# Adding four partial sums of a value row by loads that accumulate, in place of two products with a matrix of ones

## The chip, the cores and the metric

The kernel runs on one core of a Trainium2 chip. The metric is the device time of one launch in microseconds (us), lower is better. Before the change three runs took 2063.79, 2063.28 and 2062.68 us, a median of 2063.28.

## The reference, cut to what matters

One inference step of a two-layer decoder: layer A mixes tokens with a gated MLP, layer B with attention; each also has two half-weight SwiGLU blocks (the FFNs) and a gated input embedding. Everything is float32. Between the layers one shared K and V is made from the residual stream, for 512 prompt rows and for 32 "sample" rows (8 sequences of 4 new tokens). The change concerns only the sample rows of V:

```python
def shared_kv(h, kv_norm, w_kvf, b_f, k_norm):
    xs = rmsnorm(h, kv_norm)
    kvf = xs @ w_kvf
    ...
    v = kvf[..., D_ATT:2 * D_ATT].reshape(bsz, L, N_HEADS, HEAD_DIM)
    ...
k_sample, v_sample, logf_sample   # outputs; v_sample is 32 x 1024
```

`v_sample` is an output, and the attention of layer B reads it again.

## The kernel before, in words

The residual stream lies in SBUF as 8 chunks of 128 features by 544 tokens (512 prompt and 32 sample tokens side by side). A float32 product is made of three products in float32r: ScalarE (ACT) rounds an operand to its high part (line 198 for weights, 285 for activations, 297 with a gain), VectorE (DVE) subtracts to get the low part (199, 286, 298), and TensorE (PE) adds high x high (241), high x low (245) and low x high (247). Weights arrive in 512 KB blocks. All loads and stores sit in one queue in program order, SyncE's (SP), and a transfer that has to wait there keeps everything behind it waiting. A block of weights is split into its two parts two blocks ahead of its use.

The method `kv` makes K, V and the forget values. For V it goes through four groups `g` of 256 columns. In each group the prompt rows are made with the three products (829 to 831). The 32 sample rows are made in plain float32 beside them (840): for each of the 8 chunks a product with 32 rows of output, and chunk `k` writes the rows from `32 * (k % 4)` of one PSUM tile, so that four chunks fill 128 rows and the next four add to them. What stands there is four partial sums of 32 rows each; ACT copies it, times the norm, into `box["sv"]` (844). After the last group the four partial sums have to be added.

Before the change that is a product with a matrix in the constants, `C_SUM`, which has a one where the row number modulo 32 equals the column: two products of 512 columns each into PSUM tiles `t` (881), each copied by ACT into the tile `vs` (882). Two stores follow: to the output `vs` (883) and to a scratch `vsd` in device memory (884), which attention loads half a millisecond later (1260).

Behind `kv` comes the first FFN of layer B. It starts with four "plain" tiles of PE (lines 241 to 247, each copied out by 426), while ACT and DVE still make the forms of the activations (307, 311, 313, 314, 285, 286). Then it goes over to a scheme of seven products for eight (491, 24 matmuls each, order 1, 5, 6, 2, 7, 3, 4) in an order written out by hand; its evictions are lines 499 to 513, and the gate is 451 to 457. The weights of a pair of column blocks are four quarters, loaded in the order of line 165 as first to fourth; the fourth is used alone in product 2, and in the sums (line 184) for the products 3. Around the change the order within each engine comes from a scheduler that simulates the kernel.

Of the kernel before, what the change touches and what calls it, by code (L numbers as in the profile page):

```python
# [22 lines left out]
F32 = mybir.dt.float32  # L23
# [3 lines left out]
ALU = mybir.AluOpType  # L27
AX = mybir.AxisListType

P = 128  # L30
D = 1024
# [4 lines left out]
NS = NB * NQ  # L36
# [41 lines left out]
C_ID, C_ROLE, C_B4, C_H, C_SEL, C_NEGQ, C_TRI4, C_SUM = 0, 128, 140, 144, 152, 156, 160, 192  # L78
# [16 lines left out]
class Builder:  # L95
# [672 lines left out]
    def kv(self, h, box, ffn_gain):  # L768

        nc, o = self.nc, self.o  # L770
# [11 lines left out]
        box = {}  # L782
# [15 lines left out]
        def columns():  # L798

            t = self.pb()  # L800
            for j in range(4):
                nc.tensor.matmul(t[:, j:j + 1], rstd[:, j * P:(j + 1) * P], self.ident[:, 0:1], start=True, stop=True)
            for j in range(4):
                nc.tensor.matmul(t[32 * j:32 * j + 32, 4:5], rstd[:, SEQ:], self.ident[:, 0:1], start=True, stop=True,
                                 skip_group_check=True)
            box["rc"] = self.sm(5)
            nc.scalar.copy(box["rc"], t[:, 0:5])
# [61 lines left out]
        for step in KV_ORDER:  # L869
            head, _, rest = step.partition(":")  # L870
            if head == "c":
                columns()
            elif head:
                v_group(int(head[1]), parse(rest))
            else:
                for run in parse(rest)[0]:
                    run()
        vs = self.big()[:NS, :, :512]
        for a in range(2):
            t = self.pb()  # L880
            nc.tensor.matmul(t[:NS, :], self.c[:, C_SUM:C_SUM + NS], box["sv"][:, 512 * a:512 * a + 512], start=True, stop=True)
            nc.scalar.copy(vs[:, a, :], t[:NS, :])
        nc.sync.dma_start(out=o["vs"].rearrange("t (a n) -> t a n", a=2), in_=vs)
        nc.sync.dma_start(out=self.vsd[:].rearrange("t (a n) -> t a n", a=2), in_=vs)
        return nxt, rstd
# [632 lines left out]
```

## Time and profile before

| | |
|---|---|
| median of the three runs | 2063.28 us |
| the profiled execution, its own time | 2064.12 us |
| its span | 2062.4 us |
| DVE busy | 1507.2 us (73%) |
| ACT busy | 950.4 us (46%) |
| POOL (GpSimd) busy | 184.2 us (9%) |
| moved by DMA | 237.95 MB, mean 115 GB/s |

The page cuts the span into 40 slices of 51.6 us; the digits are tenths. The place of the change, around 1080 us, is at the end of slice 21, where DMA has one of its peaks: this is where V and K are stored and the next FFN's weights are fetched.

```profile
PE   8999999999999999999999999999999999999999
ACT  7534344423554344454456343534365754344451
POOL 0000000410100000043060000001141200000020
PEclk9999999999999999999999999999999999999999
DMA  5233234212223222432374323314669222222431
```

The granted clock of TensorE is full in every slice.

### The profile page before, as it was taken

What the parts mean: (1) busy time and instruction counts of PE and PEld (TensorE: products, weight loads), DVE (VectorE), ACT (ScalarE), POOL (GpSimd) and SP (SyncE); (2) the same over time, 40 slices, a digit from 0 to 9 for tenths busy, and PEclk for the clock granted to TensorE, in tenths of its full rate; (3) what the DMA queues carried; (4) which work ended last, traced back from release to release, by engine and by line L of the source; (5) the groups of instructions that cost most, each with busy time, mean ns of one, the idle gap of its engine ahead of it and who ended that gap; (6) DMA issues with size and microseconds to landing.
All of it is one profiled execution on the core that took longest, in us unless ns stands there. A gap on an engine that the chain in (4) does not pass through costs nothing.

```text
span 2062.4 us, 38838 instructions
## 1 busy us (share of the span) xinstructions
PE 2042.4 (99%) x16432; PEld 2012.4 (98%) x16432; DVE 1507.2 (73%) x1861; ACT 950.4 (46%) x1421; POOL 184.2 (9%) x222
## 2 busy tenths in 40 slices
PE   8999999999999999999999999999999999999999
PEld 8999999999999999999999999999987999999999
DVE  7877777556687778776688777786476888777773
ACT  7534344423554344454456343534365754344451
POOL 0000000410100000043060000001141200000020
PEclk9999999999999999999999999999999999999999
DMA  5233234212223222432374323314669222222431
GB/s 185 84 110 107 74 109 141 97 44 83 83 92 113 73 105 80 154 99 82 107 255 162 113 85 110 105 69 136 193 204 323 99 99 85 100 103 82 130 97 44
DMA packets 93823, 237.95 MB, mean 115 GB/s; under 512 B 9538, under 2 KB 27490, under 8 KB 93650
## 3 DMA queue, kind: packets, MB, share of 16 engines
q1 hardware_dynamic: 93506, 235.44, 34.1%
q8 instruction: 129, 2.11, 0.4%
q14 instruction: 44, 0.36, 0.1%
q10 hardware_dynamic: 144, 0.04, 0.0%
HBM read 218.95 MB, written 16.49 MB: 114 GB/s over the span
## 4 chain that ended last, share of the span: by engine, by line
PE 92%; DVE 3%; ACT 2%; issue 1%; DMA 1%; POOL 0%; SPq 0%; DVEq 0%; ACTq 0%; POOLq 0%
PE ps L491 33%; PE ps L241 16%; PE ps L247 16%; PE ps L245 16%; PE pb L491 5%; DVE big L199 1%; ACT big L198 1%; PE ps L1272 1%; PE ps L1268 1%; PE ps L1271 1%; ACT big L285 0%; DVE big L184 0%; DVE big L286 0%; PE ps L1223 0%; PE ps L829 0%
## 5 line engine op out<-in xcount | busy, mean ns | idle before, releaser
L491 PE MATMUL ps<-big,big 128*128 128x272 f32 x5616 | 727.7, 288 | 1.8 <-DVE big L508 1.3
L491 PEld LDWEIGHTS ps<-big,big 128*128 128x128 f32 x5616 | 714.2, 188 | 2.4 <-issue 1.6
L199 DVE TENSOR_TENSOR big<-big,big 128x1024 fp32r<-128x1024 f32 (+2 forms) x538 | 591.9, 1103 | 105.5 <-ACT big L198 105.0
L198 ACT CAST big<-big 128x1024 fp32r<-128x1024 f32 (+2 forms) x538 | 488.0, 932 | 267.6 <-DVE big L184 262.8
L241 PE MATMUL ps<-big,big 128*128 128x256 f32 (+1 forms) x2684 | 558.8, 289 | 7.6 <-ACT big L198 7.6
L247 PE MATMUL ps<-big,big 128*128 128x256 f32 x2684 | 554.9, 289 | 1.5 <-DVE big L199 1.5
L245 PE MATMUL ps<-big,big 128*128 128x256 f32 x2684 | 554.0, 287 | 0.0
L241 PEld LDWEIGHTS ps<-big,big 128*128 128x128 f32 x2684 | 430.9, 189 | 11.3 <-ACT big L198 8.5
L247 PEld LDWEIGHTS ps<-big,big 128*128 128x128 f32 x2684 | 429.8, 188 | 3.1 <-DVE big L199 2.7
L245 PEld LDWEIGHTS ps<-big,big 128*128 128x128 f32 x2684 | 432.5, 189 | 0.0
L326 POOL TENSOR_TENSOR st<-st,tmp 128x544 f32<-128x544 f32 (+1 forms) x63 | 87.5, 1388 | 1587.7 <-ACT tmp L324 1587.5
L530 DVE SCALAR_TENSOR_TENSOR big<-ps,big 128x544 f32<-128x544 f32 x160 | 115.6, 723 | 106.5 <-PE ps L247 106.4
L184 DVE TENSOR_TENSOR big<-big,big 128x1024 f32<-128x1024 f32 x156 | 190.2, 1219 | 0.0
L499 ACT COPY tmp<-ps 128x544 f32<-128x544 f32 x117 | 71.7, 613 | 141.2 <-PE ps L491 141.2
L454 ACT ACTIVATE big<-big 128x544 f32<-128x544 f32 x88 | 58.0, 660 | 163.2 <-DVE big L451 162.0
L491 PE MATMUL pb<-big,big 128*128 128x272 f32 x936 | 124.0, 288 | 0.0
L451 DVE TENSOR_TENSOR big<-big,st 128x1088 f32<-128x1088 f32 x88 | 113.4, 1290 | 10.6 <-ACT big L513 8.8
L491 PEld LDWEIGHTS pb<-big,big 128*128 128x128 f32 x936 | 120.2, 188 | 0.0
L286 DVE TENSOR_TENSOR big<-big,big 128x544 fp32r<-128x544 f32 (+1 forms) x112 | 82.1, 739 | 36.4 <-ACT big L285 36.3
L297 ACT ACTIVATE big<-big,gains 128x544 fp32r<-128x544 f32 (+1 forms) x80 | 55.8, 704 | 104.6 <-DVE big L530 64.9
L298 DVE SCALAR_TENSOR_TENSOR big<-big,gains,big 128x544 fp32r<-128x544 f32 (+1 forms) x80 | 65.8, 830 | 25.8 <-ACT big L297 25.8
L285 ACT CAST big<-big 128x544 fp32r<-128x544 f32 (+1 forms) x112 | 71.3, 644 | 17.8 <-DVE big L457 9.0
(208 smaller groups left out, 1430.8 us busy)
## 6 DMA issues: line engine op xcount, KB each, us to landing
big<-in_w SPq DMA_DIRECT2D x156, 512.0 KB
big<-in_w2a SPq DMA_DIRECT2D x64, 512.0 KB
big<-in_w2b SPq DMA_DIRECT2D x32, 384.0 KB
big<-in_w13p SPq DMA_DIRECT2D x16, 512.0 KB
big<-in_win SPq DMA_DIRECT2D x16, 512.0 KB
big<-in_wg SPq DMA_DIRECT2D x16, 512.0 KB
big<-in_ck SPq DMA_DIRECT2D x16, 512.0 KB
big<-in_cv SPq DMA_DIRECT2D x16, 512.0 KB
```

The lines of the kernel that those rows point to most:

```text
L184: self.nc.vector.tensor_tensor(t, a, b, ALU.add if op == "+" else ALU.subtract)
L198: self.nc.scalar.copy(hi, src)
L199: self.nc.vector.tensor_tensor(lo, src, hi.bitcast(F32), ALU.subtract)
L241: i = nc.tensor.matmul(out[:, a:b], wh, xh[:, a:b], start=s, stop=False)
L245: nc.tensor.matmul(out[:, a:b], wh, xl[:, a:b], start=False, stop=False)
L247: nc.tensor.matmul(out[:, a:b], wl, xh[:, a:b], start=False, stop=e)
L286: self.nc.vector.tensor_tensor(pair[:, 1, cols], src, pair[:, 0, cols].bitcast(F32), ALU.subtract)
L326: nc.gpsimd.tensor_tensor(acc[:, cols], acc[:, cols], sq, ALU.add)
L451: tt(g, g, rstd.unsqueeze(1).broadcast_to([P, 2, T]), ALU.mult)
L491: nc.tensor.matmul(dst[w], a[:, c], b, start=k in "152" and kp == 0 and n == 0, stop=kp == NKP - 1 and n == 2, skip_group_check=True)
L499: nc.scalar.copy(t["r" + k], t["C" if k == "5" else "A"])
L530: nc.vector.scalar_tensor_tensor(h[c], whole(out), 0.5, h[c], ALU.mult, ALU.add)
```

## The change

The two products and the two copies go. The 128 rows of `box["sv"]` are stored to a new scratch `vparts` in device memory (512 KB, SP's queue). GpSimd (POOL) then loads its four pieces of 32 rows into `vs`, one on the other: the first load overwrites, the three behind it add what they read to what is there. The stores of `vs` stay as they were.

```diff
         vs = self.big()[:NS, :, :512]
-        for a in range(2):
-            t = self.pb()
-            nc.tensor.matmul(t[:NS, :], self.c[:, C_SUM:C_SUM + NS], box["sv"][:, 512 * a:512 * a + 512], start=True, stop=True)
-            nc.scalar.copy(vs[:, a, :], t[:NS, :])
+        part = self.dram.tile([P, D], F32, name="vparts")
+        nc.sync.dma_start(out=part[:], in_=box["sv"])
+        for k in range(4):
+            src = part[NS * k:NS * k + NS, :].rearrange("t (a n) -> t a n", a=2)
+            nc.gpsimd.dma_start(out=vs, in_=src, **({"accum_op": ALU.add} if k else {}))
         nc.sync.dma_start(out=o["vs"].rearrange("t (a n) -> t a n", a=2), in_=vs)
         nc.sync.dma_start(out=self.vsd[:].rearrange("t (a n) -> t a n", a=2), in_=vs)
```

On ACT, at the end of `kv`, the program has these rows; minus marks what only the kernel before has (`big_12213` and `big_12218` are parts of V, `big_12223` is `vs`, `big_12233` the first form of the FFN's activations).

```order
 L285 CAST big_12213<-big_12038 128x512
 L285 CAST big_12218<-big_12038 128x512
-L882 COPY big_12223<-pb_12224 32x512
-L882 COPY big_12223<-pb_12227 32x512
 L307 ACTIVATE big_12233<-big_88,gains 128x544 x2
 L285 CAST big_12238<-tmp_12236 128x544
```

The two copies are gone and everything behind them moves up; no other row of ACT moves. DVE's rows are the same in both kernels. On PE the two products are gone, and the first two plain tiles are woven into each other a little differently.

On SP, at the same place, the kernel before has these rows (`big_12251`, `12321`, `12323` and `12325` are the first to fourth quarter of the first weights for the seven products; `12530` and `12568` belong to the next).

```order
L896 DMA kd<-big_12072 256x1x512
L896 DMA kd<-big_12120 256x1x512
L847 DMA out_v<-big_12038 128x512 x2
L849 DMA vd<-big_12213 256x1x512
L849 DMA vd<-big_12218 256x1x512
L883 DMA out_vs<-big_12223 64x1x512
L884 DMA vsd<-big_12223 64x1x512
L165 DMA big_12251<-in_w 128x1024
L165 DMA big_12321<-in_w 128x1024
L165 DMA big_12323<-in_w 128x1024
L165 DMA big_12325<-in_w 128x1024
L165 DMA big_12530<-in_w 128x1024
```

The changed kernel has these in their place (its line numbers are two higher behind the change).

```order
L898 DMA kd<-big_12072 256x1x512
L881 DMA vparts<-big_11362 128x1024
L898 DMA kd<-big_12120 256x1x512
L847 DMA out_v<-big_12038 128x512 x2
L849 DMA vd<-big_12213 256x1x512
L849 DMA vd<-big_12218 256x1x512
L165 DMA big_12251<-in_w 128x1024
L165 DMA big_12321<-in_w 128x1024
L165 DMA big_12323<-in_w 128x1024
L885 DMA out_vs<-big_12223 64x1x512
L886 DMA vsd<-big_12223 64x1x512
L165 DMA big_12325<-in_w 128x1024
```

The store of the partial sums stands between the two stores of K, and the two stores of `vs` have moved behind the first three quarters, ahead of the fourth. POOL has the four loads between its last copy of K's sample columns (line 893 before) and its next work, the sums of squares of line 326 at the end of the FFN.

## The prediction

> **What bounds the kernel now.** I read the page first, for the engine that sets the time.
>
> ```profile
> span 2062.4 us, 38838 instructions
> PE 2042.4 (99%) x16432; PEld 2012.4 (98%) x16432; DVE 1507.2 (73%) x1861; ACT 950.4 (46%) x1421; POOL 184.2 (9%) x222
> PE 92%; DVE 3%; ACT 2%; issue 1%; DMA 1%; POOL 0%; SPq 0%; DVEq 0%; ACTq 0%; POOLq 0%
> ```
>
> PE is busy all the time and holds 92% of the chain that ended last. So time saved on PE is worth its full size where PE is not about to wait, and nothing where it waits for another engine next. Which of the two holds at 1080 us is read from the timeline of PE, here around the two removed products (line 881) and at its next waits.
>
> ```profile
> 1063.87 1.07 PE L840 MATMUL pb<-big,xraw 128*32 128x256 f32 x16
> 1064.87 0.39 PE L829 MATMUL ps<-big,big 128*128 128x256 f32 x1
> ...
> 1076.51 1.07 PE L840 MATMUL pb<-big,xraw 128*32 128x256 f32 x16
> 1077.39 1.02 PE L881 MATMUL pb<-big,consts 128*32 128x512 f32 x2
> 1078.35 0.52 PE L241 MATMUL ps<-big,big 128*128 128x256 f32 x2
> ...
> 1080.46 0.41 PE L247 MATMUL ps<-big,big 128*128 128x256 f32 x2
> 1080.80 1.04 PE L881 MATMUL pb<-big,consts 128*32 128x512 f32 x2
> 1081.78 0.52 PE L241 MATMUL ps<-big,big 128*128 128x256 f32 x2
> 1082.13 0.42 PE L245 MATMUL ps<-big,big 128*128 128x256 f32 x2
> 1082.39 0.42 PE L247 MATMUL ps<-big,big 128*128 128x256 f32 x2
> ...
> 1092.04 0.52 PE L241 MATMUL ps<-big,big 128*128 128x256 f32 x2 [0.24 <-ACT big L198]
> ...
> 1100.03 0.52 PE L247 MATMUL ps<-big,big 128*128 128x256 f32 x2 [0.49 <-DVE big L199]
> ...
> 1105.61 9.23 PE L491 MATMUL ps<-big,big 128*128 128x272 f32 x72
> 1114.67 3.19 PE L491 MATMUL pb<-big,big 128*128 128x272 f32 x24
> ```
>
> PE runs through until 1092.04, where the third plain tile waits 0.24 us for the high part of its weights from ACT. The reader is to see that PE has almost no slack there: whatever makes PE faster before 1092 turns into a longer wait for ACT. From 1105.61 on PE runs without a wait through the first seven products. So the worth of the change is set by when ACT is done, and the timelines of ACT and of DVE show what that hangs on.
>
> ```profile
> 1085.25 1.14 ACT L285 CAST big<-big 128x512 fp32r<-128x512 f32 x2
> 1086.30 1.04 ACT L882 COPY big<-pb 32x512 f32<-32x512 f32 x2
> 1087.25 1.39 ACT L307 ACTIVATE big<-big,gains 128x544 f32<-128x544 f32 x2
> 1088.67 0.73 DVE L311 TENSOR_TENSOR tmp<-big 128x544 f32<-128x544 f32 x1 [1.47 <-ACT big L307]
> 1089.43 0.65 ACT L285 CAST big<-tmp 128x544 fp32r<-128x544 f32 x1 [0.79 <-DVE tmp L311]
> 1090.93 1.05 ACT L198 CAST big<-big 128x1024 fp32r<-128x1024 f32 x1
> 1092.02 1.23 DVE L199 TENSOR_TENSOR big<-big,big 128x1024 fp32r<-128x1024 f32 x1 [0.23 <-ACT big L198]
> ```
>
> That is a closed chain: the copies of line 882, the forms of line 307, DVE's 311 that waited 1.47 us for them, ACT's 285 that waited for it, the cast 198, and PE. The removed copies are links of it.
>
> **The change part by part.** *The two products.* A group of line 840 normally takes 1064.87 - 1063.87 = 1.00 us to the next product; with the first removed product in between it takes 1078.35 - 1076.51 = 1.84, so 0.84 goes. A step from one pair to the next is 1082.39 - 1082.13 = 0.26; with the second in between it is 1081.78 - 1080.46 = 1.32, and the pair behind it starts 0.35 later instead of 0.26, so 1.06 + 0.09 = 1.15 goes. PE gains 1.99 us. On its own that is worth nothing, since PE would stand at 1092 that much longer.
>
> *The two copies.* ACT's next instruction starts 1087.25 - 1086.30 = 0.95 us earlier. It needs nothing that moves with PE: 285 before it runs back to back with its predecessors, and the plain tiles that ACT copies out later are done 1.99 us earlier. So the chain above arrives 0.95 us earlier, PE takes up 0.95 of its 1.99 us, and waits 0.24 + 1.04 us instead of 0.24. The later wait, 1100.03, hangs on the same two engines and moves along. **The term is -0.95 us.** The different weaving of the first two tiles on PE issues the same products.
>
> *The store of the partial sums.* SP issues it behind the store of K at 1079.03, and its last piece is there when ACT has written it:
>
> ```profile
> 1078.86 0.46 ACT L844 ACTIVATE big<-pb,sm 128x256 f32<-128x256 f32 x1
> ...
> 1079.03 4.84 SPq L896 DMA_DIRECT2D kd<-big  x2
> 1087.90 0.82 SPq L883 DMA_DIRECT2D out_vs<-big  x1
> 1088.77 1.24 SPq L884 DMA_DIRECT2D vsd<-big  x1
> 1090.06 2.55 SPq L165 DMA_DIRECT2D big<-in_w  x5
> ...
> 1100.00 0.33 SPq L165 DMA_DIRECT2D big<-in_w  x1
> ```
>
> So it starts at about 1079.6. How long until it has landed, no row shows; the rows below bound it. They are windows of the DMA engines (their share is the last but one column, GB/s the last) and two transfers from the chain of waits.
>
> ```profile
> 1080.00:1085.00 5.00, 5.00 (x34) 4.01 (x34) 4.57 (x8) 4.33 (x9) 0.00 (x0) 1.00 0.99 361
> 1095.00:1100.00 5.00, 4.54 (x37) 4.32 (x35) 4.69 (x8) 4.97 (x7) 0.00 (x0) 1.00 0.75 300
> 1102.00:1103.00 1.00, 1.00 (x11) 1.00 (x10) 0.24 (x1) 0.73 (x1) 0.00 (x0) 1.00 0.77 307
> 1103.00:1104.00 1.00, 1.00 (x11) 1.00 (x10) 0.65 (x1) 0.32 (x1) 0.00 (x0) 1.00 0.04 16
> ...
> 1058.66 7.83 DMA tmp<-rows
> ...
> 1091.70 5.98 DMA big<-in_w
> ```
>
> A load of the same 512 KB that is alone, issued at 1100.00, is through by 1103.1 (the window behind it moves nearly nothing): 3.1 us. In the full stretch one took 5.98, and 272 KB behind a full queue 7.83. DMA is full at 1080 (0.99), so I take the upper end, 7.4, and the store has landed at 1087.0; the bounds are 1082.7 and 1087.4. Its 0.52 MB delay the loads behind it by at most 0.52 MB / 361 GB/s = 1.5 us, but the two stores of `vs`, 0.26 MB, no longer stand ahead of the first three quarters, and DVE did not wait for these three when it summed two of them at 1101:
>
> ```profile
> 1099.89 1.22 DVE L199 TENSOR_TENSOR big<-big,big 128x1024 fp32r<-128x1024 f32 x1
> 1101.02 1.22 DVE L184 TENSOR_TENSOR big<-big,big 128x1024 f32<-128x1024 f32 x1
> ```
>
> The load with 5.98 us, the fourth of the group, had landed by 1097.7, so there are over 3 us of cover; this costs nothing.
>
> *The four accumulating loads* are a chain: each waits for the one before it, since it adds to what that one wrote. POOL itself has nothing else queued until the end of this FFN, so nothing waits behind them there. Their duration `d` is the unknown; no load on POOL's queue is in the trace. From below, 128 KB alone takes a quarter of 3.1, 0.8 us; from above, 7.83. Nearest are 3.1 (alone) and 5.98 (in the full stretch) for four times the bytes. Three of them fall into the stretch that is full until about 1099, where 5.98 less three quarters of the bytes' own time (0.39 MB / 323 GB/s at 5.98 us, an estimate of 1.2) is 4.8; the last falls behind it, 3.1 - 1.2 = 1.9. I take d = (3 x 4.8 + 1.9) / 4 = 4.1 and the chain ends at 1087.0 + 16.4 = **1103.4**.
>
> *The wait that is added.* SP waits for that end at the first store of `vs`, and behind it in the queue stand the second store, the fourth quarter of the weights, and all that follow. In the kernel before, the fourth quarter was issued with the group of five at 1090.06; now it leaves about 1 us after the chain's end (two stores to issue, 0.82 and 1.24 us in a full queue, less in an empty one), moves behind 0.26 MB of stores (0.9 us at 307 GB/s) and takes 3.1 itself: it has landed 5.0 us after the chain's end, at 1108.4. Who waits for it is in these rows of ACT:
>
> ```profile
> 1106.32 2.00 ACT L198 CAST big<-big 128x1024 fp32r<-128x1024 f32 x2
> 1108.82 0.61 ACT L499 COPY tmp<-ps 128x544 f32<-128x544 f32 x1 [0.51 <-PE ps L491]
> ```
>
> The second cast of the pair, at 1107.27, reads the fourth quarter; moved up by 0.95 it wants it at 1106.3. So ACT and DVE stand for about 2.1 us. PE does not use that quarter before product 2, at 1114.67 - 0.95 = 1113.7, and the first thing that it misses is another: the copy of line 499 behind the cast. It saves product 1 before product 6 adds to the same PSUM tile. A product takes (1114.67 - 1105.61) / 3 = 3.02 us, so product 6 starts at 1105.61 + 6.04 - 0.95 = 1110.7; the cast and the copy take 0.95 + 0.61, so PE loses nothing as long as the quarter has landed by 1109.1, the chain has ended by **1104.1**, and d is at most 4.3. My 4.1 leaves 0.2 us per load: the cover is thin. The loads behind the fourth quarter are used later than it, and catch up.
>
> [...]
>
> **The sum** is -0.95 us against the profiled execution's own 2064.12 us. That lies 0.84 above the median of the runs shown, 2063.28, so in the runs it is 2063.28 - 0.95 = **2062.3**.
>
> **Rivals.** *The late quarter (slower).* If d is over 4.3 us, PE waits before product 6, and each 0.1 us of d costs 0.4: at d = 5.98 the stall is 4 x (5.98 - 4.3) = 6.7, net +5.8, 2069.1; at 7.83 it is 14.1, net +13.2, 2076.5. For it: DMA is full until 1099, and POOL has to prepare each load. Against it: POOL's queue does not stand behind SP's, and a load is a quarter of the size.
>
> *DVE holds POOL up.* The change is the first to let POOL make up transfers, and if POOL could not while a DVE operation of the kind at 1092.02 runs, each load would wait for the rest of one, at most 1.23 us: d = 4.1 + 1.2 = 5.3, a stall of 4.0, net +3.1, 2066.4. Against it: all DVE operations in this stretch are of two tensor inputs, and no row shows POOL held by them. [...]
>
> *PE's whole gain.* If ACT could be early by itself, PE's 1.99 us would count: 2061.3. The wait of 1.47 us for ACT's 307 speaks against it.
>
> *Nothing.* ACT and DVE stand for some microseconds and a later product takes the 0.95 us back: 2063.3.
>
> **How the numbers follow.** Chances: forecast 0.53, late quarter 0.27, DVE holds POOL 0.06, PE's whole gain 0.05, nothing 0.09. The smallest difference that a measurement of this kernel tells from no change is about 0.2%, 4.1 us. Faster by that no case gives; I leave 0.03 for what I have not seen. Slower by that needs a net of +4.1, a stall of 5.1 and d over 5.6: about half of the late quarter, 0.13. The rest, 0.84, is within. The range goes from PE's whole gain less the runs' half spread (2061.3 - 0.6 = 2060.7) to the late quarter at d = 5.98, 2069.1; it leaves out the rest of that rival and the 0.03. The likeliest case's own range is 2061.3 to 2063.3.
>
> **What would show each step.** PE's 1092.04 at about 1091.1 with a wait of 1.3 us for ACT's 198 shows the first term; POOL's four loads and the end of the last one show d; the issue of SP's first store of `vs` shows the chain's end; ACT's second cast of the pair waiting for a DMA shows the late quarter, and a wait of PE's 491 for ACT's 499 or of line 198 shows the loss. I am wrong if ACT's forms do not start earlier, or if the four loads take more than 17 us together.

## The result, and the profile after

| | before | after |
|---|---|---|
| median | 2063.38 us (19 runs) | 2066.52 us (19 runs, 2065.39 to 2068.38) |
| ratio after to before | | 1.0015, interval 1.0008 to 1.0021 |
| the profiled execution, its own time | 2064.12 us | 2065.79 us |
| its span | 2062.4 us | 2064.0 us |

The change makes the kernel slower by 3.1 us (1.7 to 4.3 by the interval). From the page of the changed kernel, its span and the engines:

```profile
span 2064.0 us, 38840 instructions
PE 2040.6 (99%) x16428; PEld 2011.7 (97%) x16428; DVE 1507.0 (73%) x1861; ACT 949.5 (46%) x1419; POOL 187.8 (9%) x226
```

PE has 1.8 us less work and the span is 1.6 us longer: PE lost more by waiting than it gained. What it waits for stands in the list of PE's waits (us in total, how often, the longest), here two rows of it, of the kernel before and then of the changed one:

```profile
PE ps L241 <- ACT big L198: 7.6, 3, 7.1
...
PE ps L491 <- ACT tmp L499: 0.5, 1, 0.5
```

```profile
PE ps L241 <- ACT big L198: 8.5, 3, 7.2
PE ps L491 <- ACT tmp L499: 2.6, 3, 1.5
```

The first row grew by 0.9. In front of the third plain tile the wait went from 0.24 to 1.01 us, so 0.77 of it is there, PE's own gain waited away; the rest lies in the first wait of the launch (its longest, 7.1 and 7.2). The wait of line 491 for line 499 grew by 2.1: new waits among the products of seven. The timeline of PE after the change shows where they are:

```profile
1090.43 0.52 PE L241 MATMUL ps<-big,big 128*128 128x256 f32 x2 [1.01 <-ACT big L198]
...
1104.00 6.20 PE L491 MATMUL ps<-big,big 128*128 128x272 f32 x48
1111.69 3.30 PE L491 MATMUL ps<-big,big 128*128 128x272 f32 x24 [1.49 <-ACT tmp L499]
...
1118.65 6.29 PE L491 MATMUL ps<-big,big 128*128 128x272 f32 x48 [0.64 <-ACT tmp L499]
1125.43 12.26 PE L491 MATMUL ps<-big,big 128*128 128x272 f32 x96 [0.48 <-DVE big L508]
1137.53 3.16 PE L491 MATMUL pb<-big,big 128*128 128x272 f32 x24
```

In the kernel before, all these products ran without a wait. These rows follow those that the prediction shows:

```profile
1117.70 18.20 PE L491 MATMUL ps<-big,big 128*128 128x272 f32 x144
1135.74 3.16 PE L491 MATMUL pb<-big,big 128*128 128x272 f32 x24
```

Two executions do not start this stage at the same moment, so a fixed point ahead of the change is needed. DVE's first operation of line 311 in this stage is one: it precedes all that the copies touch. Here it is in the kernel before, and then after the change, there with the rows in which ACT and DVE miss the fourth quarter:

```profile
1079.62 0.71 DVE L311 TENSOR_TENSOR tmp<-big 128x544 f32<-128x544 f32 x1
```

```profile
1078.97 0.71 DVE L311 TENSOR_TENSOR tmp<-big 128x544 f32<-128x544 f32 x1
...
1110.08 1.05 ACT L198 CAST big<-big 128x1024 fp32r<-128x1024 f32 x1 [4.32 <-DMA big<-in_w]
1111.03 0.61 ACT L499 COPY tmp<-ps 128x544 f32<-128x544 f32 x1
...
1111.16 1.23 DVE L199 TENSOR_TENSOR big<-big,big 128x1024 fp32r<-128x1024 f32 x1 [4.14 <-DMA big<-in_w]
```

The whole stage stands 0.65 us earlier in this execution (1079.62 - 1078.97), and the first product of seven 1.61 (1105.61 - 1104.00), so 0.96 is gained up to there. The last product shown is 1.79 later instead (1137.53 - 1135.74): 3.40 us were lost on the way, and 2.44 net. (The three waits of PE shown above add up to 2.61 only, because a wait counts from the modelled end of the row before it; the starts of the rows hold the whole loss.) ACT and DVE stand for over 4 us before a transfer, and PE waits for the copy 499 behind it. Why the quarter is late is to be read on POOL's and SP's timelines:

```profile
1087.65 0.78 POOL L884 DMA_DIRECT2D big<-vparts  x1 [10.98 <-DMA vparts<-big]
1094.38 0.86 POOL L884 DMA_DIRECT2D big<-vparts  x1 [5.95 <-DMA big<-vparts]
1097.91 0.81 POOL L884 DMA_DIRECT2D big<-vparts  x1 [2.68 <-DMA big<-vparts]
1101.82 0.81 POOL L884 DMA_DIRECT2D big<-vparts  x1 [3.10 <-DMA big<-vparts]
...
1079.89 0.93 SPq L881 DMA_DIRECT2D vparts<-big  x1
...
1087.23 2.66 SPq L165 DMA_DIRECT2D big<-in_w  x3
1104.96 0.66 SPq L885 DMA_DIRECT2D out_vs<-big  x1
...
1106.31 4.00 SPq L165 DMA_DIRECT2D big<-in_w  x5
```

SP issues three quarters at 1087.23, then stands until the fourth load has landed, 1104.96, and only then issues the two stores and the fourth quarter. The store of the partial sums took 1087.65 - 1079.89 = 7.8 us; the loads, from one issue to the next, 6.73, 3.53, 3.91 and, to SP's store, 3.14, together 17.3.

### The profile page after: what moved, and what is told of

Read it like the earlier page. It is cut to its first block, busy times and chain, and to the rows that moved or that the text cites. A ratio compares the mean times of both kernels' runs of the same rounds, so it can differ in the third digit from the quotient of the medians.

```text
span 2064.0 us, 38840 instructions
## 1 busy us (share of the span) xinstructions
PE 2040.6 (99%) x16428; PEld 2011.7 (97%) x16428; DVE 1507.0 (73%) x1861; ACT 949.5 (46%) x1419; POOL 187.8 (9%) x226
## 4 chain that ended last, share of the span: by engine, by line
PE 92%; DVE 3%; ACT 2%; DMA 1%; issue 1%; POOL 0%; SPq 0%; ACTq 0%; DVEq 0%; POOLq 0%
PE ps L491 32%; PE ps L241 16%; PE ps L247 16%; PE ps L245 16%; PE pb L491 5%; DVE big L199 1%; ACT big L198 1%; PE ps L1274 1%; PE ps L1270 1%; PE ps L1273 1%; DVE big L184 1%; PE ps L1225 0%; PE ps L829 0%; PE ps L830 0%; ACT big L285 0%
```

## The experiments

**Theory.** The loss is the late quarter: its place in SP's queue behind a wait for the loads. **Rivals:** the added traffic, or DVE held up by POOL's making up the transfers (POOL's four rows of them last 0.78 to 0.86 us each); and, for the size of the gain, that PE's own 1.99 us count.

All runs were timed against the kernel before on the same chip. The table has, from the timelines, the start of DVE's first 311 of the stage, of the first product of seven (491) and of the last 491 block shown above, and the distance from the 311 to the two.

| kernel | median us | ratio to before, interval | 311 | first 491 | last block | 311 to first 491 | 311 to last block |
|---|---|---|---|---|---|---|---|
| before | 2063.4 to 2063.5 | | 1079.62 | 1105.61 | 1135.74 | 25.99 | 56.12 |
| the change | 2066.52 | 1.0015 (1.0008 to 1.0021) | 1078.97 | 1104.00 | 1137.53 | 25.03 | 58.56 |
| e1, stores by POOL | 2062.34 | 0.9996 (0.9987 to 1.0005) | 1079.60 | 1104.64 | 1134.77 | 25.04 | 55.17 |
| e9, the same again | 2062.64 | 0.9998 (0.9989 to 1.0007) | 1078.34 | 1103.38 | 1133.51 | 25.04 | 55.17 |
| e2, traffic only | 2063.59 | 0.9999 (0.9990 to 1.0008) | 1079.17 | 1105.16 | 1135.30 | 25.99 | 56.13 |
| e7, two loads | 2065.83 | 1.0013 (1.0004 to 1.0023) | 1078.66 | 1103.71 | 1136.28 | 25.05 | 57.62 |
| e3, no sum | 2063.46 | 1.0000 (0.9991 to 1.0009) | 1077.91 | 1102.96 | 1133.09 | 25.05 | 55.18 |
| e5, products only | 2063.55 | 0.9999 (0.9990 to 1.0008) | 1078.68 | 1103.72 | 1133.85 | 25.04 | 55.17 |
| e6, copies only | 2064.10 | 1.0004 (0.9995 to 1.0013) | 1079.32 | 1107.00 | 1137.13 | 27.68 | 57.81 |
| e8, POOL copies | 2065.14 | 1.0008 (0.9999 to 1.0017) | 1079.96 | 1105.84 | 1135.97 | 25.88 | 56.01 |

**e1 and e9: the stores of `vs` on another queue.** POOL issues them behind its loads; SP does not wait for these, and its next eight loads of weights stand in one row, from 1087.86 on.

```diff
-        nc.sync.dma_start(out=o["vs"].rearrange("t (a n) -> t a n", a=2), in_=vs)
-        nc.sync.dma_start(out=self.vsd[:].rearrange("t (a n) -> t a n", a=2), in_=vs)
+        nc.gpsimd.dma_start(out=o["vs"].rearrange("t (a n) -> t a n", a=2), in_=vs)
+        nc.gpsimd.dma_start(out=self.vsd[:].rearrange("t (a n) -> t a n", a=2), in_=vs)
```

> The changed kernel, but the two stores of the summed rows are issued by POOL behind the four loads, so SP's queue does not wait for them; on SP the fourth quarter of the weights stands right behind the third again. Theory 'late quarter' (the loss comes only from SP waiting for the chain of loads ahead of the fourth quarter): ACT's second cast does not wait for a DMA, no stall of PE behind 1104, and the 0.95 us of the removed copies are left: 2063.4 - 0.95 = 2062.4. Rival 'traffic' (the loss comes from 1 MB more of transfers in a stretch where DMA is full): the same bytes move, so the time stays at about 2066.5. Rival 'POOL' (making up the transfers holds DVE up): also about 2066.5.

> The changed kernel with the two stores of vs issued by POOL, a second time, to settle the size of its gain: 2062.3 if the first term is real and the late quarter the only loss (first run 2062.34), 2063.4 if the first run was noise.

The loads and their traffic are as in the change, and the loss is gone: 2062.34 and 2062.64, as the late quarter has it. POOL's, ACT's and PE's timelines of e1:

```profile
1106.56 0.55 POOL L885 DMA_DIRECT2D out_vs<-big  x1 [2.45 <-DMA big<-vparts]
...
1105.35 2.00 ACT L198 CAST big<-big 128x1024 fp32r<-128x1024 f32 x2
...
1104.64 9.23 PE L491 MATMUL ps<-big,big 128*128 128x272 f32 x72
...
1116.73 18.20 PE L491 MATMUL ps<-big,big 128*128 128x272 f32 x144
```

The loads end even later here, at 1106.56 (the 311 stands 0.63 later than in the change), but ACT's pair of casts runs through without a wait, and none of PE's products of seven waits. This version is some 4 us faster than the change. Against the kernel before it shows 1.1 and 0.9 us less; both intervals take in no change, so it is not shown to beat that kernel, though the stage itself is 0.95 shorter in both profiles.

**e2: the traffic alone.** The kernel before, with the store and the four loads added into a buffer that nobody reads.

```diff
+        vx = self.big()[:NS, :, :512]
+        part = self.dram.tile([P, D], F32, name="vparts")
+        nc.sync.dma_start(out=part[:], in_=box["sv"])
+        for k in range(4):
+            src = part[NS * k:NS * k + NS, :].rearrange("t (a n) -> t a n", a=2)
+            nc.gpsimd.dma_start(out=vx, in_=src, **({"accum_op": ALU.add} if k else {}))
```

> The kernel before, with its products, copies and stores, and beside them the store of the partial sums and the four accumulating loads into a tile that nobody reads. Theory 'late quarter': nobody waits for these transfers, so the time is that of before, 2063.4 within 0.5. Rivals 'traffic' and 'POOL': 3.1 us from the changed kernel plus the 0.95 that the copies cost here, 2067.5.

2063.59, and the stage has the length of before to 0.01 us. Neither the bytes nor POOL's work beside DVE cost anything here. Both rivals of the loss would have made it 2067.5, which lies above the interval (up to 2065.0), and they fall. Whether the loads themselves take longer because of DVE this run cannot tell, since nobody waits for them.

**e7: a shorter chain in a worse place.** Two loads instead of four, so two of the four partial sums are left out.

```diff
-        for k in range(4):
+        for k in range(2):
```

> The changed kernel with two of the four loads, so two of the four partial sums are left out. The chain is then 7 us shorter, but the scheduler puts the two stores of the sum behind the first quarter of the weights on SP, so the second and third quarter wait for it. By the trace of the changed kernel the chain ends at 1097.9, the third quarter lands at about 1104.3, and DVE, which wants to sum it at 1099.4, waits 4.9 us. Theory 'late quarter' (what counts is where the wait stands in SP's queue and who needs what is behind it): PE loses 2 to 3.5 us again, 2064.5 to 2066. Rivals 'traffic' and 'POOL' (what counts is the number of loads): about half of the changed kernel's loss of 4.1, 2064.5 at most, and no wait of DVE for a DMA.

SP's, DVE's and PE's timelines:

```profile
1086.91 0.82 SPq L165 DMA_DIRECT2D big<-in_w  x1
1096.36 0.66 SPq L885 DMA_DIRECT2D out_vs<-big  x1
...
1102.97 1.23 DVE L184 TENSOR_TENSOR big<-big,big 128x1024 f32<-128x1024 f32 x1 [3.77 <-DMA big<-in_w]
...
1110.27 3.30 PE L491 MATMUL ps<-big,big 128*128 128x272 f32 x24 [0.36 <-ACT tmp L499]
...
1117.41 6.29 PE L491 MATMUL ps<-big,big 128*128 128x272 f32 x48 [0.81 <-ACT tmp L499]
```

The chain ends 8.3 us sooner than in the change (1104.96 - 1096.36, less the 0.31 by which this execution stands earlier at the 311), but the scheduler, which knows that it is shorter, has put the stores behind the first quarter, so that three quarters wait instead of one. The loss stays: 2065.83. The time alone would not rule out the rivals' 2064.5, which the interval just takes in, but DVE's wait of 3.77 us for a quarter does; the late quarter had put it at 4.9. What counts is what stands behind the wait, not how much is loaded.

**e3: no sum at all.** Products and copies go, and nothing comes in their place.

```diff
-        vs = self.big()[:NS, :, :512]
-        for a in range(2):
...
+        vs = box["sv"][:NS, :].rearrange("t (a n) -> t a n", a=2)
```

> The kernel before without the two products and the two copies, and without anything in their place: the stores take the first 32 rows of the partial sums, so the addition of the four sums is left out. This is the whole gain there is. By the first term of the prediction (ACT's two copies lie in the chain, PE's own time does not count): -0.95, 2062.4. If PE's own 1.99 us count: 2061.4. If later waits take it back: 2063.4.

A miss: 2063.46, no gain in the median, although the stage is 0.95 shorter from the 311 on. The interval, 1.9 us to each side, takes in a gain of 0.95 as well as none, so the runs alone cannot tell. The next two were made to find out more.

**e5: the products alone,** without the copies.

```diff
-        vs = self.big()[:NS, :, :512]
+        vs = box["sv"][:NS, :].rearrange("t (a n) -> t a n", a=2)
         for a in range(2):
...
-            nc.scalar.copy(vs[:, a, :], t[:NS, :])
```

> The kernel before without the two copies on ACT; the two products with the matrix of ones stay on PE and nobody reads them, and the stores of vs take the first of the four partial sums straight from box["sv"] (the addition is left out). My theory, that the copies are worth 0.95 us through ACT and PE's products nothing: the first seven-product matmul 0.9 to 1.0 us earlier against line 840's last, and 2062.4 us. Rival (PE's own work counts): no gain, 2063.4. If the place gains 0.95 and the time does not, as in the run without products and copies, the gain is lost again later.

The stage is 0.95 shorter with the products still on PE: the copies are the gain, PE's 1.99 us are not. But again the median shows none, 2063.55. Half a millisecond later the scheduler has exchanged two rows on DVE, in e3, e5 and e8 alike and in no other kernel of the table: in attention a reciprocal stands ahead of the next reduction. DVE and then PE, first of the kernel before, then of e5:

```profile
1506.04 0.87 DVE L1123 TENSOR_REDUCE sm<-ps 128x1 f32<-128x256 f32 x2
...
1509.26 0.44 PE L1105 MATMUL ps<-big,big 128*128 128x384 f32 x1 [0.49 <-ACT tmp L1124]
```

```profile
1504.15 0.41 DVE L1122 TENSOR_REDUCE sm<-ps 128x1 f32<-128x256 f32 x1
1505.18 0.16 DVE L1124 RECIPROCAL sm<-sm 128x1 f32<-128x1 f32 x1 [0.63 <-ACT tmp L1123]
1505.26 0.54 DVE L1122 TENSOR_REDUCE sm<-ps 128x1 f32<-128x384 f32 x1
...
1508.16 0.46 PE L1104 MATMUL ps<-big,big 128*128 128x384 f32 x1 [1.27 <-ACT tmp L1123]
```

The reciprocal waits for ACT, the reduction that could run stands behind it, and PE waits 1.27 us instead of 0.49. Counted from the 311, which stands 0.94 earlier in e5, the first row of DVE is 0.95 earlier than before, and PE's row only 0.16. That gives 0.8 of the 0.95 back. In e1, whose rows are not exchanged, the same product of PE stands at 1508.29 with a wait of 0.48, still 0.95 earlier. It is read from the profiles; none of the three kernels was run with the two rows put back.

**e6: the copies alone,** from SBUF instead of PSUM, without the products.

```diff
-            t = self.pb()
-            nc.tensor.matmul(t[:NS, :], self.c[:, C_SUM:C_SUM + NS], box["sv"][:, 512 * a:512 * a + 512], start=True, stop=True)
-            nc.scalar.copy(vs[:, a, :], t[:NS, :])
+            nc.scalar.copy(vs[:, a, :], box["sv"][:NS, 512 * a:512 * a + 512])
```

> The kernel before without the two products on PE; the two copies on ACT stay, but copy the first of the four partial sums from SBUF (the addition is left out). My theory: PE's 1.99 us turn into a longer wait for ACT at the third plain tile (0.24 + 1.99 = about 2.2 us, less what the copies themselves move), the first seven-product matmul where it was, 2063.4 us. Rival (PE's whole gain): 2061.4.

Not only is PE's whole gain absent (2064.10; 2061.4 lies below the interval): the stage, expected as long as before, is 1.69 us longer. PE's timeline, then the windows (the last but two column is the granted clock, then DMA's share and GB/s):

```profile
1091.83 0.82 PE L241 MATMUL ps<-big,big 128*128 128x256 f32 x2 [2.39 <-ACT big L198]
...
1097.79 0.66 PE L241 MATMUL ps<-big,big 128*128 128x256 f32 x2
1098.24 0.46 PE L245 MATMUL ps<-big,big 128*128 128x256 f32 x2
...
1092.00:1095.00 3.00, 3.00 (x12) 2.69 (x13) 2.43 (x3) 2.71 (x5) 0.00 (x0) 0.50 0.98 384
...
1098.50:1101.00 2.50, 2.50 (x22) 2.50 (x21) 2.46 (x3) 0.96 (x2) 0.00 (x0) 1.00 0.13 23
```

PE waits 2.39 us, about the 2.2 that were expected, and then runs at half its clock until about 1098.3, a pair in 0.45 us instead of 0.25. In this execution PE's saved work is worth less than nothing, because it turns into a wait behind which PE runs at a granted clock of 0.50. The runs alone, with an interval that takes in no change, do not show the loss.

**e8: the buffer kept.** POOL copies the first partial sum into `vs`, so that buffers rotate as before.

```diff
+        nc.gpsimd.tensor_copy(vs, box["sv"][:NS, :].rearrange("t (a n) -> t a n", a=2))
```

> No products and no copies on ACT; POOL copies the first of the four partial sums into vs, so that the buffers rotate as in the kernel before and only PE's and ACT's rows differ (the addition is left out). If the 0.95 us are real and the run without a vs buffer lost them through other buffers or by noise: 2062.4. If the gain is always lost again after the FFN: 2063.4.

Both expectations missed: 2065.14. The experiment brought a cost of its own, seen on POOL's and DVE's timelines:

```profile
1079.73 1.20 POOL L879 COPY big<-big 32x1024 f32<-32x1024 f32 x1 [2.07 <-ACT big L844]
...
1079.96 1.55 DVE L311 TENSOR_TENSOR tmp<-big 128x544 f32<-128x544 f32 x1
```

The 311 takes 1.55 us instead of 0.71 while POOL copies. Of the 25.88 in the table 0.84 is that; without it 25.04 is left, as in e1, e3, e5 and e9. And it has the exchanged rows in attention. The shorter stage (0.11) and the exchange (0.8) together make 0.7 of the 1.6 us by which its median lies above the kernel before; the rest has no cause shown, and its interval takes in no change. So it does not decide whether a changed rotation of buffers costs anything; that stays open.

## Why the prediction was wrong, step by step

The forecast was 0.95 us less than before, 2062.3; the runs show 3.1 more, 2066.5. That this lies inside the range is no merit of the likeliest case: the range went up to 2069.1 for the late quarter's sake. Two steps failed. The chain of loads was to end at 1103.4, with 0.7 us of cover, and it ended 2.2 later: this turned a gain into a loss. And one stall was to be the whole loss, with everything catching up behind it: this made the loss 3.4 us instead of 1.5. The runs also told the two kernels apart at 0.15%, where the prediction took 0.2% for the smallest difference that they could.

**The first term was right in place and size.** From the 311 to the first product of seven 0.95 was forecast; 0.96 was measured, and in six of the seven kernels without the copies the distance lies between 25.03 and 25.05 against 25.99 (the seventh, e8, has a cost of its own). PE's row at 1092.04 came as foretold, at 1090.43 (0.65 of the difference is the offset), with a wait of 1.01 for line 198 instead of 1.28. That the products themselves are worth nothing is shown by e5, which keeps them and gains the same.

**The end of the chain was the step that failed.** On the clock of the kernel before (0.65 added) it was put at 1103.4 and came at 1105.61. Of the 2.2 us, 1.3 lie in the store of the partial sums, which landed at 1088.3 instead of 1087.0: it was issued 0.9 later than assumed and took 7.8 instead of 7.4. The other 0.9 lie in the loads, 17.3 us instead of 16.4. That their mean, d = 4.33, is so near the 4.1 is luck in part: the four errors, +1.9, -1.3, -0.9 and +1.2, cancel for the most part. The first load, issued 0.4 us behind the three quarters (1087.23), took 6.73 instead of 4.8. The next two took less than 4.8, and the stretch that I took for full was not: the change itself held the fourth quarter and what follows back, as a window of the DMA engines shows (share 0.41, 64 GB/s). The last took 3.14 instead of 1.9.

```profile
1095.00:1100.00 5.00, 4.51 (x36) 4.30 (x35) 4.69 (x7) 3.56 (x5) 1.04 (x2) 1.00 0.41 64
```

**The bound was right.** PE was to lose nothing if the chain ended by 1104.1, that is if the loads took no more than 17 us. The chain ended 1.5 later, and PE's first new wait is 1.49. Quarter and chain were 5.0 apart in the forecast and are 5.1 in the trace (1110.08 - 1104.96).

**The size of the loss was not.** After the stall at product 6 the prediction had everything catch up, since the loads behind are used later. The loads did: up to the last product shown, ACT and DVE have no second wait for a DMA. DVE did not. Of the kernel before, these windows lie behind the stall (behind the length come the busy times of PE, of its weight loads and of DVE, each with its count):

```profile
1117.00:1123.00 6.00, 6.00 (x50) 6.00 (x50) 6.00 (x8) 2.43 (x3) 0.00 (x0) 1.00 0.08 32
...
1129.00:1135.00 6.00, 6.00 (x51) 6.00 (x50) 5.87 (x8) 4.07 (x7) 0.00 (x0) 1.00 0.00 0
```

DVE is busy for 6.00 and 5.87 of 6 us there, and for 5.96 in the window between them. What it stood for before the quarter it cannot make up there. Its operation 508, for which PE waits at 1125.43, shows it, before and then after the change:

```profile
1121.99 0.72 DVE L508 TENSOR_TENSOR big<-ps,tmp 128x544 f32<-128x544 f32 x1
```

```profile
1124.56 0.72 DVE L508 TENSOR_TENSOR big<-ps,tmp 128x544 f32<-128x544 f32 x1
```

With the 0.65 that is 3.2 us later, long behind the stall, and PE ran into it again, at 1118.65 (there through ACT's 499) and at 1125.43. The loss became 3.4 us instead of 1.5, and -0.95 + 3.4 = +2.4 in the profiles beside +3.1 in the runs, whose interval takes in 2.4. By the prediction's own sum the measured end of the chain would have given only -0.95 + 1.5 = +0.55.

**The rivals.** That the traffic, or POOL's work beside DVE, costs time by itself is excluded by e1 and e2. "DVE holds POOL up" is another thing, longer loads, and no run tests it alone. Its price for a load, 5.3, is not what the last three took, 3.53, 3.91 and 3.14, although DVE was busy for 4.69 of 5.00 us in the window above; for the first, with 6.73, it stays open beside the traffic of the three quarters. That its time, 2066.4, is so near the measured one is chance. No run shows that the two tensor inputs of DVE's operations speak against it, as the prediction had it: such an operation did run 0.84 us longer beside a copy of POOL (e8). "PE's whole gain" is excluded by e5 and e6. "Nothing" had the right picture of an engine that stands and hands its lateness on, but took it for smaller than the gain. The late quarter was the right one, and e1 shows it by its removal; its chance of 0.27 was too low for a bound with 0.7 us of cover on a sum of two unseen durations.

## What to carry to other kernels

When a transfer's data come from a slow chain, look at what stands behind it in the same in-order queue, and give such a store a queue on which nobody waits: here that alone was worth 4 us. A cover that is thinner than the spread of the durations it rests on is no cover: here 0.7 us, with loads between 3.14 and 6.73. A stall of an engine that has no idle time behind it was handed on at later places as well, here 3.4 us instead of 1.5 with DVE busy for 5.87 to 6.00 of 6 us in the kernel before, so look at that engine's share in the windows after the stall. When a small edit is timed under a scheduler, compare the order of rows in the whole program, since it can exchange two rows half a millisecond away and give most of the gain back there, 0.8 of 0.95 us in e5.

## What the runs showed that was not expected

Behind a wait of PE of 2.39 us (e6) the granted clock was 0.50 for some 6 to 7 us: it is 1.00 in the window from 1089 to 1091.5, 0.50 in those from 1092 to 1095 and from 1095 to 1098, and 1.00 again in that from 1098.5 to 1101. After 1.49 in the changed kernel (1.00 from 1111.7 to 1118) and after 1.65 in e8 (1.00 from 1092.3 to 1098), whose row stands here, no such stretch followed:

```profile
1092.26 0.52 PE L241 MATMUL ps<-big,big 128*128 128x256 f32 x2 [1.65 <-ACT big L198]
```

It is one wait in one execution, and the runs do not show from what length of a wait on this happens, or whether the length decides it.

While POOL copied for 1.20 us in e8, DVE's 311 took 1.55 us instead of 0.71, so 0.84 longer; it began 0.97 us before the copy's end. Through it the copy held up the chain that PE waits for: 25.88 us from the 311 to the first product of seven, instead of 25.04. It is one copy in one execution. Beside the loads that POOL issued nothing of the kind shows: in the changed kernel the two operations of line 199 beside the third load took 2.36 us together, as before, and the stage of e2 has 56.13 us against 56.12.
